# Which engine makes the low halves of the streamed weights: VectorE in place of VectorE and GpSimd in turn

## The chip, the cores and the metric

The kernel runs on one core of a Trainium2 chip. Its time is device microseconds (us) from launch to end. Before the change the median of 3 runs was 2225.28 us (2224.88 to 2227.35). One further execution was profiled and took 2224.93 us. All durations below come from that one.

The engines are named as in the profile: PE is TensorE (PEld its weight loads), DVE is VectorE, ACT is ScalarE, POOL is GpSimd and SP is the engine that issues the loads.

## The reference

Two transformer blocks run on one sequence of 256 tokens with 1024 features, in fp32. The first has two layers: a short-convolution mixer, then windowed attention, each followed by a product-key mixture of experts (PEER). The second block mixes pooling, an mLSTM and a block attention, and ends with a gated feed-forward. The change touches the first convolution mixer and that feed-forward:

```python
def _short_conv_mixer(x, w_in, w_conv, w_out):
    gate_b, gate_c, h = jnp.split(x @ w_in, 3, axis=-1)
    y = conv(gate_c * h, w_conv)          # depthwise, width 3
    return (gate_b * y) @ w_out

# feed-forward of the second block: D_FF = 2816 = 22 * 128
h2 = rmsnorm(x, ln2_g)
u = causal_dwconv(h2 @ w_up, ffn_conv)    # depthwise, width 3
x = x + (silu(u[..., :D_FF]) * u[..., D_FF:]) @ w_down
```

## The kernel before

**Split weights.** Every fp32 weight comes from HBM once, in units of 128 x 1024 (512 KB). Each unit is split into two fp32r tiles: ACT copies `raw` to the high part `wh` (L127), and one of DVE and POOL subtracts, `wl = raw - wh` (L128). The activations are split alike (`xh`, `xl`; `ah`, `al` for the feed-forward's inner values, L186 and L187). A product is then three matmuls into one bank: high by high, high by low, low by high.

**Two shapes of product.** `c_unit` (L153) takes one unit as eight 128 x 128 blocks that stand still while 256 token columns move: 24 matmuls (L159 to L161). `t_mm` (L172) takes a unit as the moving operand, 512 columns at a time, over four banks: 12 matmuls (L177, L178, L181). `t_end` (L204) does the last two units of such a sum in halves (L168 to L170), so that the first half of the tokens ends early.

**Buffers.** `raw` has four, `wh` and `wl` three each. `prepare` (L149) splits up to the third unit behind the one just used, so the split of a unit can start when PE has used up the unit three before it.

**Who makes the low part.** `lo_on["pat"]` is a string, and a counter steps through it: "V" is DVE always, "P" POOL always, "VP" each in turn. Stages set it. Before the change it is "VP" in the convolution mixer (from the end of its first step on) and in the feed-forward. `settle` (one split, L272) and `t_end` override it with "P", and `t_phase` with "V".

**The order.** PE and SP follow the order in which the program is written. The instructions of DVE, ACT and POOL are put in order by the scheduler of the tile layer when the kernel is built. Each engine works through its own list strictly in order.

**The feed-forward.** Step c of 25 makes two `c_unit`s, one for each half of the gate (banks 0 and 1 for even c, 2 and 3 for odd c), and from step 3 on one `t_mm` with the gated result of step c - 3. `up_work` does the work between: for each half a scale by `rbc` that reads the bank (L1136) and three taps (L1139, L1140, L1141), then Silu on ACT (L1143) and the product (L1144). `split_small` splits that product (L186, L187). A full step therefore uses three weight units, and half of their low parts (1.5 on average) are POOL's. Ahead of it, `norm_scales` and `spread` make `rbc`: two DVE scalings of the identity (L328), two matmuls (L329) and a copy (L330).

**The convolution mixer.** Eight steps of three `c_unit`s; `conv_work` (L377 to L384) is its DVE work, seven instructions a step.

Of the kernel before, what the change touches and what calls it, by code (L numbers as in the profile page):

```python
# [40 lines left out]
def kernel(ctx: ExitStack, tc: tile.TileContext, a, out):  # L41
    nc = tc.nc
    V, S, P, T = nc.vector, nc.scalar, nc.gpsimd, nc.tensor
# [48 lines left out]
    lo_on = {"i": 0, "pat": "V"}  # L92
# [60 lines left out]
    def c_unit(out_ps, ahead=True, src=None):  # L153
        h, l = unit()
        ah, al = src or (xh, xl)
        hv = h.rearrange("p (k m) -> p k m", k=8)
        lv = l.rearrange("p (k m) -> p k m", k=8)
        for k in range(8):
            T.matmul(out_ps, hv[:, k], ah[:, k], start=k == 0, stop=False)  # L159
            T.matmul(out_ps, hv[:, k], al[:, k], start=False, stop=False)  # L160
            T.matmul(out_ps, lv[:, k], ah[:, k], start=False, stop=k == 7)  # L161
        if ahead:
            prepare()
# [40 lines left out]
    def t_end(k, n, get, cur, arrive):  # L204

        pat, lo_on["pat"] = lo_on["pat"], "P"
        prepare()
        lo_on["pat"] = pat
        u = [unit()]
        while len(cur) < 2:  # L210
            cur.append(get(k + len(cur)))
        u.append(unit())

        def part(b, nn, q):
            t_half(bank[4 + b * 2 + nn], u[q][0], u[q][1], cur[q][0], cur[q][1], b, nn, k == 0 and q == 0, q == 1)

        for nn in range(2):
            part(0, nn, 0)
            part(0, nn, 1)
        for nn in range(2):  # L220
            arrive(0, nn)
            part(1, nn, 0)
        for nn in range(2):
            part(1, nn, 1)
        for nn in range(2):
            arrive(1, nn)
# [38 lines left out]
    def landing(scale=None, low=False):  # L265
        def arrive(b, n):
            add_x(b, n, scale)
            for c in range(4 * n, 4 * n + 4):
                T.transpose(spot(b, c, low), x[:, b, c * 128:c * 128 + 128], ident)
        return arrive  # L270

    def settle(g, low=False, dst=None):  # L272

        h, l = dst or (xh, xl)
        for b in range(2):
            bs = slice(b * 128, b * 128 + 128)
            for c in range(8):
                i = S.activation(h[:, c, bs], spot(b, c, low), AF.Copy, scale=g[:, c:c + 1])
                V.scalar_tensor_tensor(l[:, c, bs], spot(b, c, low), g[:, c:c + 1], h[:, c, bs],  # L279
                                       op0=ALU.mult, op1=ALU.subtract)  # L280
            if b == 0:
                pat, lo_on["pat"] = lo_on["pat"], "P"
                pump_split(st["use"] + 2)
                lo_on["pat"] = pat
        st["after"] = i
# [79 lines left out]
    def conv_norm():  # L365
        norm_scales()
        spread(bank[7])
        V.tensor_tensor(rb2, rbc, rbc, op=ALU.mult)
# [6 lines left out]
    def conv_work(ct):  # L375
        bs = 4 - 4 * (ct % 2)
        V.tensor_tensor(csb, bank[bs + 1][:, :256], rb2, op=ALU.mult)  # L377
        V.tensor_tensor(u[:, 1:257], bank[bs + 2][:, :256], csb, op=ALU.mult)
        w = [cols[:, C_CONVW + ct * 3 + k:C_CONVW + ct * 3 + k + 1] for k in range(3)]
        V.tensor_scalar(ysb, u[:, 0:256], w[0], None, op0=ALU.mult)  # L380
        V.scalar_tensor_tensor(ysb, u[:, 1:257], w[1], ysb, op0=ALU.mult, op1=ALU.add)
        V.scalar_tensor_tensor(ysb, u[:, 2:258], w[2], ysb, op0=ALU.mult, op1=ALU.add)
        V.tensor_tensor(ysb, ysb, rbc, op=ALU.mult)
        V.tensor_tensor(G[ct], bank[bs][:, :256], ysb, op=ALU.mult)  # L384

    for ct in range(8):
        for g in range(3):
            c_unit(bank[4 - 4 * (ct % 2) + g][:, :256])
            if g == 0 and ct:
                conv_work(ct - 1)  # L390
        if ct == 0:
            lo_on["pat"] = "VP"
            conv_norm()
            T.matmul(bank[3][0:32, :], rb, bk1, start=True, stop=True)
            V.tensor_tensor(mk1, bank[3][0:32, :], mk1, op=ALU.add)
# [399 lines left out]
    def block2():  # L795
# [322 lines left out]
        wo(5)  # L1118
        fetch(7)
        t_end(6, 8, None, cur, landing())  # L1120
        lo_on["pat"] = "VP"
        settle(cols[:, C_LN2:C_LN2 + 8])


# [54 lines left out]
    attention()  # L1179
    peer(1)  # L1180
    block2()


# [120 lines left out]
```

## Time and profile before

| | before |
|---|---|
| median of 3 runs | 2225.28 us |
| profiled execution | 2224.93 us, span 2223.2 us |
| PE busy | 2140.8 us (96%) |
| DVE busy | 1698.7 us (76%) |
| ACT busy | 1144.2 us (51%) |
| POOL busy | 520.7 us (23%) |
| low parts (L128) on DVE | 494, mean 1228 ns |
| low parts (L128) on POOL | 197, mean 2556 ns |
| mean granted TensorE clock | 0.985 |

The span is 1.7 us shorter than the time of the same execution. A share over the whole span mixes stages with different limits: the convolution mixer stands at about 8 to 105 us and the feed-forward at about 2007 to 2219 us, and what matters is read from those two. An engine with a high busy share is not thereby doing useful work all that time: an instruction counts as busy from its start to its end, also while it is held up.

### The profile page before, as it was taken

How to read it: one execution, taken by the hardware profiler on the slowest of the kernel's cores; microseconds unless marked ns; L12 is line 12 of the kernel's file. 1: busy time of each engine (PE TensorE's matmuls, PEld its weight loads, DVE VectorE, ACT ScalarE, POOL GpSimd, SP SyncE). 2: the span in 40 equal slices, each digit the busy share in tenths (PEclk: the TensorE clock that was granted, in tenths of full speed). 3: DMA queues.
4: the chain of work that ended last, by engine and by line, in shares of the span. 5: the costliest groups of instructions: out<-in, count | busy, mean ns of one | idle time of the engine just before them, and what ended most of it. 6: DMA issues, size and time to landing. Idle time of an engine off the chain costs nothing.

```text
span 2223.2 us, 38284 instructions
## 1 busy us (share of the span) xinstructions
PE 2140.8 (96%) x14590; PEld 1945.2 (87%) x14590; DVE 1698.7 (76%) x3048; ACT 1144.2 (51%) x2102; POOL 520.7 (23%) x219
## 2 busy tenths in 40 slices
PE   9999799999999999989998999999999999889998
PEld 9899799999988888877988999998888887768887
DVE  7699968896566666686999788955666666889998
ACT  4455345554555555666544555545555556655333
POOL 3368630000000000144678100000000003533443
PEclk9999899999999999999998999999999999999999
DMA  7686454555667666534454554556676665424553
GB/s 226 181 239 188 133 178 152 155 159 171 205 204 225 209 191 197 173 103 152 144 160 152 166 158 153 156 178 209 196 219 194 193 193 176 124 88 153 168 170 125
DMA packets 109025, 384.45 MB, mean 173 GB/s; under 512 B 11876, under 2 KB 15332, under 8 KB 108584
## 3 DMA queue, kind: packets, MB, share of 16 engines
q1 hardware_dynamic: 108552, 381.81, 55.3%
q8 instruction: 114, 1.87, 0.3%
q14 instruction: 71, 0.58, 0.1%
q10 hardware_dynamic: 288, 0.19, 0.0%
HBM read 374.61 MB, written 7.34 MB: 172 GB/s over the span
## 4 chain that ended last, share of the span: by engine, by line
PE 80%; DVE 12%; issue 4%; POOL 2%; ACT 2%; DMA 0%; SPq 0%; POOLq 0%; ACTq 0%; DVEq 0%
PE bank L159 14%; PE bank L161 13%; PE bank L160 13%; PE bank L177 11%; PE bank L178 11%; PE bank L181 11%; PE bank L533 3%; DVE arena L1141 2%; POOL wl L128 2%; DVE wl L128 2%; DVE arena L1139 1%; ACT wh L127 1%; DVE arena L1140 1%; DVE arena L858 1%; DVE arena L1136 1%
## 5 line engine op out<-in xcount | busy, mean ns | idle before, releaser
L127 ACT ACTIVATE wh<-raw 128x1024 fp32r<-128x1024 f32 x691 | 729.6, 1059 | 370.0 <-PE bank L160 185.5
L159 PE MATMUL bank<-xh,wh 128*128 128x256 f32 x2792 | 808.9, 290 | 18.7 <-ACT arena L554 11.3
L161 PE MATMUL bank<-xh,wl 128*128 128x256 f32 x2792 | 797.3, 286 | 12.4 <-DVE wl L128 10.2
L160 PE MATMUL bank<-xl,wh 128*128 128x256 f32 x2792 | 794.7, 285 | 0.0
L128 DVE TENSOR_TENSOR wl<-raw,wh 128x1024 fp32r<-128x1024 f32 x494 | 606.5, 1228 | 244.5 <-ACT wh L127 244.3
L128 POOL TENSOR_TENSOR wl<-raw,wh 128x1024 fp32r<-128x1024 f32 x197 | 501.7, 2556 | 1051.4 <-ACT wh L127 1000.1
L159 PEld LDWEIGHTS bank<-xh,wh 128*128 128x128 f32 x2792 | 540.1, 193 | 24.6 <-ACT arena L554 12.1
L161 PEld LDWEIGHTS bank<-xh,wl 128*128 128x128 f32 x2792 | 539.6, 193 | 18.7 <-DVE wl L128 13.8
L160 PEld LDWEIGHTS bank<-xl,wh 128*128 128x128 f32 x2792 | 540.5, 194 | 1.5 <-DVE xl L279 0.8
L177 PE MATMUL bank<-wh,ah 128*128 128x512 f32 x1160 | 454.6, 392 | 0.0
L178 PE MATMUL bank<-wl,ah 128*128 128x512 f32 x1160 | 454.1, 391 | 0.2 <-DVE wl L128 0.2
L181 PE MATMUL bank<-wh,al 128*128 128x512 f32 x1160 | 358.2, 390 | 0.0
L186 ACT ACTIVATE ah<-arena 128x256 fp32r<-128x256 f32 x270 | 112.7, 418 | 341.7 <-PE bank L178 279.2
L178 PEld LDWEIGHTS bank<-wl,ah 128*128 128x128 f32 x1160 | 218.8, 189 | 47.6 <-DVE wl L128 2.7
L177 PEld LDWEIGHTS bank<-wh,ah 128*128 128x128 f32 x1160 | 218.8, 189 | 46.6 <-issue 2.1
L181 PEld LDWEIGHTS bank<-wh,al 128*128 128x128 f32 x1160 | 218.5, 188 | 45.8
L187 DVE TENSOR_TENSOR al<-arena,ah 128x256 fp32r<-128x256 f32 x270 | 116.2, 431 | 125.0 <-PE bank L181 110.1
L310 POOL TENSOR_TENSOR top<-x,arena 128x512 f32<-128x512 f32 x4 | 5.1, 1293 | 631.9 <-DVE x L245 631.9
L524 DVE TENSOR_TENSOR x<-iota,ijT 128x1024 f16<-128x1024 f16 x128 | 89.9, 703 | 52.9 <-PE bank L533 52.9
L547 ACT ACTIVATE arena<-bank 128x284 f32<-128x284 f32 (+42 forms) x128 | 38.9, 304 | 130.9 <-DVE arena L545 130.9
L526 DVE TENSOR_TENSOR x<-x,wT 128x1024 f16<-128x1024 f16 x128 | 96.6, 756 | 0.0
L533 PE MATMUL bank<-x 128*128 128x128 f16 x1024 | 81.2, 220 | 0.0
(296 smaller groups left out, 2056.8 us busy)
## 6 DMA issues: line engine op xcount, KB each, us to landing
raw<-in_u_dram SPq DMA_DIRECT2D x256, 512.0 KB, 3.5
raw<-in_v_dram SPq DMA_DIRECT2D x256, 512.0 KB, 3.5
raw<-in_ff_dram SPq DMA_DIRECT2D x66, 512.0 KB, 3.5
raw<-in_wq_dram SPq DMA_DIRECT2D x32, 512.0 KB, 4.0
raw<-in_conv_in_dram SPq DMA_DIRECT2D x23, 512.0 KB, 4.1
raw<-in_conv_out_dram SPq DMA_DIRECT2D x8, 512.0 KB, 3.6
f_d<-arena SPq DMA_DIRECT2D x8, 512.0 KB, 7.2
raw<-in_aq_dram SPq DMA_DIRECT2D x8, 512.0 KB, 3.5
```

The lines of the kernel that those rows point to most:

```text
L127: S.activation(h, r, AF.Copy)
L128: (P if pat[lo_on["i"] % len(pat)] == "P" else V).tensor_sub(l, r, h)
L159: T.matmul(out_ps, hv[:, k], ah[:, k], start=k == 0, stop=False)
L160: T.matmul(out_ps, hv[:, k], al[:, k], start=False, stop=False)
L161: T.matmul(out_ps, lv[:, k], ah[:, k], start=False, stop=k == 7)
L177: T.matmul(bank[4 + b * 2 + n], sh[:, bs], h[:, ns], start=first, stop=False)
L178: T.matmul(bank[4 + b * 2 + n], sh[:, bs], l[:, ns], start=False, stop=False)
L181: T.matmul(bank[4 + b * 2 + n], sl[:, bs], h[:, ns], start=False, stop=last)
L186: S.activation(h, src, AF.Copy)
L187: V.tensor_sub(l, src, h)
L526: V.tensor_tensor(W, E[:, 1:2].to_broadcast(shape), wT[:, c, :, :, None, :].to_broadcast(shape), op=ALU.mult)
L533: T.matmul(bk[:, t * 128:t * 128 + 128], E[:, 0, t // 2, :, t % 2], W[:, q, t // 2, :, t % 2], start=q == 0, stop=q == 1)
```

## The change

Two settings of the pattern change. The one of the convolution mixer is taken out, so that the pattern keeps its first value "V"; the one ahead of the feed-forward becomes "V".

```diff
         if ct == 0:
-            lo_on["pat"] = "VP"
             conv_norm()
...
         t_end(6, 8, None, cur, landing())
-        lo_on["pat"] = "VP"
+        lo_on["pat"] = "V"
         settle(cols[:, C_LN2:C_LN2 + 8])
```

Since a line falls away, the lines after L391 have a number lower by one in the new kernel: its L1138 is the L1139 of before.

In the DVE's list the last full step of the feed-forward (`up_work(21)`, banks 2 and 3) stood like this; `wl` is a low part of a weight unit, `al` that of the activations, `arena` the working memory:

```order
2404 L1136 TENSOR_TENSOR arena<-bank_94,rbc 128x256
2405 L1139 TENSOR_SCALAR arena<-arena,cols 128x256
2406 L1140 SCALAR_TENSOR_TENSOR arena<-arena,cols 128x256
2407 L1141 SCALAR_TENSOR_TENSOR arena<-arena,cols 128x256
2408 L1136 TENSOR_TENSOR arena<-bank_95,rbc 128x256
2409 L1139 TENSOR_SCALAR arena<-arena,cols 128x256
2410 L1140 SCALAR_TENSOR_TENSOR arena<-arena,cols 128x256
2411 L128 TENSOR_TENSOR wl<-raw,wh 128x1024
2412 L1141 SCALAR_TENSOR_TENSOR arena<-arena,cols 128x256
2413 L1144 TENSOR_TENSOR arena<-arena 128x256
2414 L187 TENSOR_TENSOR al<-arena,ah 128x256
```

In the new list the same step, from its second instruction on, is:

```order
2448 L1138 TENSOR_SCALAR arena<-arena,cols 128x256
2449 L1139 SCALAR_TENSOR_TENSOR arena<-arena,cols 128x256
2450 L128 TENSOR_TENSOR wl<-raw,wh 128x1024
2451 L1140 SCALAR_TENSOR_TENSOR arena<-arena,cols 128x256
2452 L1135 TENSOR_TENSOR arena<-bank_95,rbc 128x256
2453 L1138 TENSOR_SCALAR arena<-arena,cols 128x256
2454 L128 TENSOR_TENSOR wl<-raw,wh 128x1024
2455 L1139 SCALAR_TENSOR_TENSOR arena<-arena,cols 128x256
2456 L1140 SCALAR_TENSOR_TENSOR arena<-arena,cols 128x256
2457 L1143 TENSOR_TENSOR arena<-arena 128x256
2458 L128 TENSOR_TENSOR wl<-raw,wh 128x1024
2459 L187 TENSOR_TENSOR al<-arena,ah 128x256
```

Every step now has three low parts in the DVE's list: one between the taps of the first half, one between those of the second, and one between the product and `al`. Before, steps had two and one in turn.

On POOL, the end of the list was as follows (L1015 to L1018 are the pooling mixer):

```order
19 L1015 TENSOR_TENSOR top<-top 64x256
20 L1016 COPY top<-top 64x256
21 L1017 TENSOR_TENSOR top<-top,arena 128x2x256
22 L1018 TENSOR_TENSOR top<-top,arena 128x2x256
23 L128 TENSOR_TENSOR wl<-raw,wh 128x1024 x33
```

and is now:

```order
19 L1014 TENSOR_TENSOR top<-top 64x256
20 L1015 COPY top<-top 64x256
21 L1016 TENSOR_TENSOR top<-top,arena 128x2x256
22 L1017 TENSOR_TENSOR top<-top,arena 128x2x256
23 L128 TENSOR_TENSOR wl<-raw,wh 128x1024
```

32 of the 33 low parts have left POOL; the one that stays is `settle`'s. Near the start of the same list a run of 143 becomes one of 132: 11 low parts of the convolution mixer have left as well. In that mixer, two steps of the DVE's list were:

```order
34 L384 TENSOR_TENSOR arena<-bank_96,arena 128x256
35 L187 TENSOR_TENSOR al<-arena,ah 128x256
36 L377 TENSOR_TENSOR arena<-bank_93,arena 128x256
37 L128 TENSOR_TENSOR wl<-raw,wh 128x1024
38 L378 TENSOR_TENSOR arena<-bank_94,arena 128x256
39 L380 TENSOR_SCALAR arena<-arena,cols 128x256
40 L381 SCALAR_TENSOR_TENSOR arena<-arena,cols 128x256
41 L382 SCALAR_TENSOR_TENSOR arena<-arena,cols 128x256
42 L383 TENSOR_TENSOR arena<-arena,rbc 128x256
43 L384 TENSOR_TENSOR arena<-bank_92,arena 128x256
44 L128 TENSOR_TENSOR wl<-raw,wh 128x1024
45 L187 TENSOR_TENSOR al<-arena,ah 128x256
```

and are now:

```order
34 L128 TENSOR_TENSOR wl<-raw,wh 128x1024
35 L384 TENSOR_TENSOR arena<-bank_96,arena 128x256
36 L377 TENSOR_TENSOR arena<-bank_93,arena 128x256
37 L128 TENSOR_TENSOR wl<-raw,wh 128x1024
38 L187 TENSOR_TENSOR al<-arena,ah 128x256
39 L378 TENSOR_TENSOR arena<-bank_94,arena 128x256
40 L380 TENSOR_SCALAR arena<-arena,cols 128x256
41 L381 SCALAR_TENSOR_TENSOR arena<-arena,cols 128x256
42 L128 TENSOR_TENSOR wl<-raw,wh 128x1024
43 L382 SCALAR_TENSOR_TENSOR arena<-arena,cols 128x256
44 L383 TENSOR_TENSOR arena<-arena,rbc 128x256
45 L384 TENSOR_TENSOR arena<-bank_92,arena 128x256
```

A low part has moved in ahead of the last product (L384), and one between the taps. The lists of PE and SP are the same as before; ACT's holds the same instructions, some of the feed-forward's in another order.

## Rows read from the trace of the kernel before

**Rows 1.** Stretches: length, busy us and count of each engine, granted clock, DMA.

```profile
core 0: us, PE busy (x) PEld busy (x) DVE busy (x) ACT busy (x) POOL busy (x), PEclk, DMA share, GB/s
20.00:82.00 62.00, 62.00 (x510) 60.99 (x509) 47.03 (x69) 23.52 (x25) 24.41 (x10) 1.00 0.62 185
...
2018.00:2031.90 13.90, 13.90 (x118) 13.90 (x117) 13.87 (x27) 6.82 (x10) 5.12 (x2) 1.00 0.46 152
2034.70:2195.80 161.10, 150.96 (x1021) 136.93 (x1020) 151.26 (x202) 63.02 (x86) 66.40 (x27) 1.00 0.54 167
2195.80:2208.00 12.20, 11.78 (x74) 10.10 (x73) 11.62 (x17) 4.17 (x7) 5.47 (x2) 1.00 0.29 88
2208.00:2219.20 11.20, 7.78 (x25) 5.40 (x24) 6.44 (x7) 1.29 (x2) 2.44 (x1) 0.85 0.12 47
2212.60:2217.50 4.90, 4.86 (x14) 3.80 (x15) 1.81 (x3) 0.00 (x0) 0.00 (x0) 0.65 0.15 56
```

**Rows 2.** Waits from 2034.7 us on: waiter, whom for, us, times, longest.

```profile
PEld bank L161 <- DVE wl L128: 13.8, 18, 0.9
...
PEld bank L168 <- ACT ah L186: 3.1, 1, 3.1
```

**Rows 3.** Groups by line, 2034.7 to 2195.8 us: busy us, mean ns.

```profile
L128 POOL TENSOR_TENSOR wl<-raw,wh 128x1024 fp32r<-128x1024 f32 x27 | 71.9, 2663 | 99.4 <-ACT wh L127 58.1 <-DVE al L187 32.7 <-DVE arena L1139 4.8
...
L1141 DVE SCALAR_TENSOR_TENSOR arena<-arena,cols 128x256 f32<-128x256 f32 x35 | 49.0, 1399 | 0.6
L128 DVE TENSOR_TENSOR wl<-raw,wh 128x1024 fp32r<-128x1024 f32 x26 | 31.7, 1221 | 1.8 <-ACT wh L127 1.8
...
L1139 DVE TENSOR_SCALAR arena<-arena,cols 128x256 f32<-128x256 f32 x35 | 27.0, 772 | 1.1
...
L1140 DVE SCALAR_TENSOR_TENSOR arena<-arena,cols 128x256 f32<-128x256 f32 x36 | 23.5, 653 | 1.1
...
L1136 DVE TENSOR_TENSOR arena<-bank,rbc 128x256 f32<-128x256 f32 x34 | 14.2, 417 | 0.0
...
L1144 DVE TENSOR_TENSOR arena<-arena 128x256 f32<-128x256 f32 x18 | 7.6, 424 | 1.2
L187 DVE TENSOR_TENSOR al<-arena,ah 128x256 fp32r<-128x256 f32 x18 | 7.6, 422 | 4.0 <-ACT ah L186 3.9
```

**Rows 4.** Single lines, 2034.7 to 2195.8 us: shortest, median and longest ns.

```profile
L1141 DVE SCALAR_TENSOR_TENSOR arena<-arena,cols x35: 470/485/2626, 2035.7 to 2190.3; 128x256 f32<-128x256 f32 x35
...
L1139 DVE TENSOR_SCALAR arena<-arena,cols x35: 342/354/2196, 2035.4 to 2194.6; 128x256 f32<-128x256 f32 x35
...
L1140 DVE SCALAR_TENSOR_TENSOR arena<-arena,cols x36: 473/485/2616, 2033.2 to 2195.0; 128x256 f32<-128x256 f32 x36
```

**Rows 5.** Timelines of POOL and DVE near the end: start us, duration us.

```profile
2195.77 3.11 POOL L128 TENSOR_TENSOR wl<-raw,wh 128x1024 fp32r<-128x1024 f32 x1 [3.17 <-ACT wh L127]
...
2196.55 2.62 DVE L1141 SCALAR_TENSOR_TENSOR arena<-arena,cols 128x256 f32<-128x256 f32 x1
...
2202.94 2.40 POOL L128 TENSOR_TENSOR wl<-raw,wh 128x1024 fp32r<-128x1024 f32 x1 [4.06 <-DVE al L187]
...
2203.30 2.18 DVE L1139 TENSOR_SCALAR arena<-arena,cols 128x256 f32<-128x256 f32 x1
```

**Rows 6.** PE's timeline over the last units.

```profile
2205.28 0.39 PE L177 MATMUL bank<-wh,ah 128*128 128x512 f32 x1
...
2208.01 0.47 PE L168 MATMUL bank<-wh,ah 128*128 128x512 f32 x1
...
2212.64 0.51 PE L168 MATMUL bank<-wh,ah 128*128 128x512 f32 x1 [2.66 <-ACT ah L186]
...
2218.94 0.40 PE L170 MATMUL bank<-wh,al 128*128 128x512 f32 x1
```

**Rows 7.** Timelines of DVE and PE where `rbc` is made.

```profile
2016.61 0.28 DVE L328 TENSOR_SCALAR gt<-ident,sm 128x128 f32<-128x128 f32 x1
...
2017.12 0.61 PE L329 MATMUL bank<-gt,ones 128*128 128x128 f32 x4
```

**Rows 8.** One tap of the convolution mixer: shortest, median, longest ns.

```profile
L382 DVE SCALAR_TENSOR_TENSOR arena<-arena,cols x8: 481/1494/2587, 25.8 to 83.7; 128x256 f32<-128x256 f32 x8
```

## The prediction

> **What bounds the kernel now.** First the stretches [rows 1], since the two stages that change have different limits. In the convolution mixer (20 to 82 us) PE is busy for all 62.0 us and DVE for 47.0: PE is the limit, and it waits for no one. In the feed-forward (2034.7 to 2195.8 us, 17 steps, 1020 matmuls) PE is busy 151.0 of 161.1 us and DVE 151.3: here DVE is as full as PE, and PE has gaps. Next, who causes them: PE's weight loads of L161 wait 13.8 us in 18 waits for a low part that DVE makes, and behind the last step one wait of 3.1 us is for ACT's `ah` [rows 2]. So the feed-forward is bound by DVE. POOL's own low parts are hardly ever waited for.
>
> Then, what fills DVE [rows 3, 4]. The tap L1141 takes 485 ns in the median and 2626 ns at most; L1139 354 and 2196; L1140 485 and 2616. The same instruction on the same shape is either short or some 2 us longer. The timelines say when [rows 5]: POOL's low part runs from 2195.77 to 2198.88, and L1141 from 2196.55 to 2199.17, done 0.29 us after POOL. POOL's next runs from 2202.94 to 2205.34, and L1139 from 2203.30 to 2205.48, done 0.14 us after it. A tap that begins while POOL subtracts ends when POOL ends. L1136, which reads a bank, has a mean of 417 ns and is never long [rows 3].
>
> The sum of the stretching: L1141 49.0 - 35 x 0.485 = 32.0 us, L1139 27.0 - 35 x 0.354 = 14.6, L1140 23.5 - 36 x 0.485 = 6.0, together 52.6 us of DVE time. POOL's group holds 27 instructions, one cut off by the edge of the stretch, so 26 to 27 share it: 2.0 us each. A low part that DVE makes itself costs it 1.221 us [rows 3]. Taken from DVE to POOL to spare DVE 1.2 us, a low part costs DVE 2.0.
>
> The Trainium skill has a rule for this, in "SBUF — State Buffer", section "Who interferes with whom": a DVE instruction with two inputs in SBUF, or in a two-port mode, and a GpSimd instruction that reads SBUF exclude each other, and the one that comes second is blocked until the first is done. By that rule L1136, with one input in PSUM, should escape and the taps should not, and the trace agrees (417 ns mean against 2626 at most). Another of its rules speaks against the change: "Perfetto Trace Analysis", section "Optimizing Scalar/DVE Operations", says that where DVE is saturated, handing work to ScalarE or even GpSimd may make sense. By that rule alone, taking work back to a DVE that is busy 151 of 161 us makes the kernel slower; that is the last rival below. The same section adds that between these two engines it might not help.
>
> **The change, part by part.** *DVE in the feed-forward.* A full step now holds three low parts. From the short durations [rows 3, 4]: two halves at 0.417 + 0.354 + 0.485 + 0.485 = 1.741 us make 3.48; the product 0.424 and `al` 0.422 make 0.85; three low parts at 1.221 make 3.66. That is 7.99 us. What PE needs for a step: in 2018.0 to 2031.9 us, where it runs without a gap, 118 matmuls (two of them cut by the edges, so 116) take 13.9 us, 0.120 each [rows 1]; the 12 matmuls of a `t_mm` take from 2205.28 to 2208.01, 0.2275 each [rows 6]. 48 x 0.120 + 12 x 0.2275 = 5.76 + 2.73 = 8.49 us. The step of before took 161.1 / 17 = 9.48. DVE at 7.99 falls below PE at 8.49, so PE becomes the limit, with 0.5 us of a step to spare on DVE.
>
> *Steady steps:* 17 x (9.48 - 8.49) = 16.8 us go. *The last step and the product behind it* (2195.80 to 2208.00): 48 x 0.120 + 24 x 0.2275 = 11.22 us against 12.20, so 1.0 us.
>
> *The tail.* From 2208.01 to the last matmul at 2218.94 there are 23 intervals [rows 6]; at 0.2275 they would take 5.23 us, and took 10.93. The 5.7 us are the wait for the low part of unit 64, the 2.66 us for `ah` of the last product, and the clock behind that wait: granted 0.65 on average from 2212.6 to 2217.5 us [rows 1], so between its two levels of 1.2 and 2.4 GHz, after PE had stood still. These waits exist because DVE is behind. When it is not, the last chain starts with the last `c_unit`: L1136 0.42, L1139 0.35, low part 1.22, L1140 and L1141 0.97, product 0.42, then `ah` on ACT. That is 3.4 us plus what ACT has ahead of it in its list, the high part of the last unit, which cannot start before PE has left the unit three earlier, 2.73 us behind the `c_unit`; so `ah` comes at about 4.3 us. PE wants it after two `t_mm`s and three matmuls, 27 x 0.2275 = 6.1 us. It is 1.8 us early, so the whole tail goes: 5.7 us. The clock has then no standstill to fall for.
>
> *What is added.* Ahead of `rbc` one more low part (unit 3's) stands in DVE's list. The second L328 ended at 2016.89 and PE came to L329 at 2017.12 [rows 7]: cover of 0.23 us. PE then waits between 0 (where the low part falls into time in which DVE waited anyway) and 1.22 - 0.23 = 1.0 us; I take the middle, 0.5. After that DVE starts some steps late, as it does now, and with 0.5 us a step to spare it catches up only over many; a few waits for a low part will remain in the first steps. Their bounds are 0 and, at the 0.77 us of a wait now (13.8 / 18), one per step for five steps, 3.9 us. I take 1.4, a little nearer to the lower end, since the low parts are made two units ahead of their use (about 5.7 us) and a delay under 3 us costs nothing.
>
> What is queued behind a low part that waits for ACT's `wh`: the next tap, Silu and the product, and for these PE waits only three steps later. DVE waited 1.8 us in all for `wh` in the whole stretch [rows 3]. The loads of `raw` are set free by the subtraction, which on DVE ends sooner than on POOL; three units of 0.524 MB in 8.49 us are 185 GB/s, and the mixer already draws 185 [rows 1]. I cost it at nothing.
>
> *Convolution mixer.* DVE gets 11 low parts, 13.4 us, and loses the stretching (L382 alone has a median of 1494 ns against a shortest of 481, [rows 8]), about 2.0 us for each. It stays near 47 of 62 us and PE near 62 of 62: 0, bounds 0 (PE has no wait to win) and 2 us (two low parts late by one subtraction each).
>
> **The sum:** 16.8 + 1.0 + 5.7 = 23.5 us less; 0.5 + 1.4 = 1.9 us more; net 21.6. From the profiled 2224.93 us this gives 2203.3. The median is 0.35 us above the profiled time, so 2203.7; I say 2204. A measurement tells 0.2%, 4.5 us, from no change.
>
> **The rivals.**
> *The tail stays.* ACT's list puts high parts ahead of Silu and `ah` at the end; if the last chain is late by more than its 1.8 us, PE waits again and the clock falls again. For it: the margin is that of one low part and a half. Against it: each piece is priced from rows. It gives 2203.7 + 5.7 = 2209.4. Chance 0.15.
> *Half the gain.* DVE's 0.5 us a step is eaten by waits for `wh`, by its order: a mean of 0.33 us for each of three low parts takes DVE to 8.98 us, half of the way back to 9.48, and the tail stays too. 2203.7 + 8.4 + 5.7 - 1.4 = 2216. For it: three waits a step where there were 1.5. Against it: 1.8 us of such waits over 26 now, 0.07 each. Chance 0.08.
> *No change.* The gaps come back as waits for ACT or a load: 2225. Against it: ACT is busy 63.0 of 161.1 us and DMA 0.54 [rows 1]. Chance 0.03. That the change does nothing is excluded by POOL's list, which is 43 low parts shorter.
> *Slower.* The long taps are DVE's own, because each follows a low part, and do not go with POOL's work. Then DVE adds 26 x 1.221 = 31.7 us to 151.3 and needs 183 us where 161.1 were: 22 us more, and about 2 for the steps around, 2249. This decides from the point where a subtraction taken off POOL gives DVE back less than the 1.22 us it costs there; rows say 2.0. For it: L1141 does stand behind a low part in [rows 5]. Against it: L1139 in the same rows does not, and both end with POOL's instruction. Chance 0.05.
>
> **How the numbers follow.** The forecast, 0.69, has a range of its own from 2202 (nothing left over: 2225.28 - 23.5) to 2207 (both added terms at their upper bounds). To hold 8 in 10 the range must take in the first rival and its remainders: 2202 to 2211. Faster by over 0.2%: forecast 0.69, tail 0.15, half 0.08, less a little for what lies near the bound, 0.91. Same 0.04, slower 0.05.
>
> **What would show it.** Right: no tap of 2 us in the feed-forward; DVE busy about 130 us (151.3 - 52.6 + 31.7) over 17 steps of about 8.5 us; PE's waits for a low part of DVE nearly gone; no wait of PE for `ah` at the end, and a granted clock of 1.0 through the tail; the mixer's stretch unchanged with PE at 62 of 62. Wrong: taps that stay long with POOL idle, a row of waits of DVE for `wh`, or low parts on DVE that take over 1.4 us.

## The result: 1.1% faster, as forecast

| | before | changed |
|---|---|---|
| median | 2226.20 us (5 runs) | 2203.01 us (5 runs) |
| range | 2224.88 to 2227.35 | 2201.73 to 2204.09 |
| profiled span | 2223.2 us | 2200.0 us |
| PE busy | 96% | 97% |
| DVE busy | 1698.7 us | 1675.0 us |
| POOL busy | 520.7 us | 409.1 us |

The ratio is 0.9892, with a 95% interval of 0.9880 to 0.9903: 23.2 us less, where 21.6 was worked out and 2204 forecast. DVE has 43 instructions more and is busy for 24 us less.

The stretches of the changed kernel that answer to [rows 1] (columns as there: length, then PE, PEld, DVE, ACT and POOL busy with counts, granted clock, DMA). The feed-forward's stretches end earlier and hold the same matmuls:

```profile
20.00:82.00 62.00, 62.00 (x511) 61.04 (x511) 49.46 (x79) 23.80 (x25) 0.00 (x0) 1.00 0.60 190
...
2034.70:2179.20 144.50, 144.50 (x1022) 136.16 (x1021) 130.99 (x230) 65.51 (x88) 0.00 (x0) 1.00 0.60 187
2179.20:2190.50 11.30, 11.30 (x74) 10.34 (x73) 10.14 (x18) 5.16 (x7) 0.00 (x0) 1.00 0.18 53
2190.50:2196.20 5.70, 5.63 (x25) 4.32 (x23) 2.31 (x5) 0.00 (x0) 0.00 (x0) 1.00 0.24 92
```

Read against [rows 1] one stretch at a time. The mixer (20 to 82 us): PE 62.0 of 62.0 in both, nothing won, nothing lost. The 17 steps: 161.1 us before, 144.5 now, 8.50 a step, with PE busy throughout. The last step: 12.2 and 11.3. The tail: 11.2 and 5.7, at a clock of 1.00 where 0.85 was granted. Together 16.6 + 0.9 + 5.5 = 23.0 us of the span's 23.2.

The lines of the taps, shortest, median and longest ns (numbers lower by one than in [rows 4]):

```profile
L1138 DVE TENSOR_SCALAR arena<-arena,cols x35: 345/353/356, 2035.8 to 2177.2; 128x256 f32<-128x256 f32 x35
...
L1139 DVE SCALAR_TENSOR_TENSOR arena<-arena,cols x36: 473/480/488, 2035.4 to 2178.9; 128x256 f32<-128x256 f32 x36
...
L1140 DVE SCALAR_TENSOR_TENSOR arena<-arena,cols x37: 474/480/486, 2035.0 to 2176.3; 128x256 f32<-128x256 f32 x37
```

The medians are within 5 ns of those of [rows 4]; the long ones are gone. The instructions have the same shapes and operands; what changed is POOL's work beside them and their place among the low parts. The waits from 2034.7 us on (waiter, whom for, total us, times, longest; "issue" where the profile shows no one that was waited for) are no longer PE's on DVE, as in [rows 2]:

```profile
ACT wh L127 <- issue: 55.3, 38, 1.5
ACT wh L127 <- PE bank L160: 26.3, 15, 1.8
DVE wl L128 <- ACT wh L127: 7.8, 33, 0.6
...
DVE arena L1135 <- PE bank L161: 2.9, 15, 0.5
...
ACT ah L186 <- DVE arena L1143: 0.3, 1, 0.3
```

Where the profile names someone, ACT waits for PE to give back a weight buffer, and DVE waits for ACT's high part and for PE's banks; PE itself is busy for all 144.5 us. That is what a PE-bound stage looks like: the others are ahead and held back by PE.

### The profile page after: what moved, and what is told of

The parts are those of the page before. It is cut to its first block, busy times and chain, and to the rows that moved or that the text cites. A ratio compares the mean times of both kernels' runs of the same rounds, so it can differ in the third digit from the quotient of the medians.

```text
span 2200.0 us, 38262 instructions
## 1 busy us (share of the span) xinstructions
PE 2131.1 (97%) x14590; PEld 1943.2 (88%) x14590; DVE 1675.0 (76%) x3091; ACT 1145.7 (52%) x2102; POOL 409.1 (19%) x176
## 4 chain that ended last, share of the span: by engine, by line
PE 88%; DVE 5%; issue 3%; POOL 2%; ACT 1%; DMA 1%; POOLq 0%; SPq 0%; ACTq 0%
PE bank L159 15%; PE bank L161 15%; PE bank L160 15%; PE bank L177 12%; PE bank L178 12%; PE bank L181 12%; PE bank L532 3%; POOL wl L128 2%; DVE arena L857 1%; ACT wh L127 1%; PE bank L429 0%; DMA x_d<-x 0%; PE bank L735 0%; DVE x L243 0%; DVE wl L128 0%
## 5 line engine op out<-in xcount | busy, mean ns | idle before, releaser
L128 DVE TENSOR_TENSOR wl<-raw,wh 128x1024 fp32r<-128x1024 f32 x537 | 659.1, 1227 | 256.0 <-ACT wh L127 255.3
L159 PE MATMUL bank<-xh,wh 128*128 128x256 f32 x2792 | 808.9, 290 | 19.0 <-ACT arena L553 11.3
L128 POOL TENSOR_TENSOR wl<-raw,wh 128x1024 fp32r<-128x1024 f32 x154 | 390.4, 2547 | 959.7 <-ACT wh L127 957.7
L546 ACT ACTIVATE arena<-bank 128x284 f32<-128x284 f32 (+42 forms) x128 | 38.8, 303 | 131.0 <-DVE arena L544 131.0
```

The lines of the kernel that those rows point to most:

```text
L128: (P if pat[lo_on["i"] % len(pat)] == "P" else V).tensor_sub(l, r, h)
```

## The experiments

The theory: a subtraction on POOL holds up a DVE instruction that reads two inputs from SBUF, or a TENSOR_SCALAR from SBUF to SBUF such as L1139 of before (one input, 2196 ns at most), for some 2.0 us, which costs time where DVE limits. The expectations call the second case the two-port mode; the runs show that it is held, not in which mode it ran. The rivals: the gain is a matter of DVE's new order; POOL's low parts were late as such; DVE's long taps were its own.

### Which of the two places: the mixer or the feed-forward

```diff
 # e1_mixer_only, against the changed kernel: the feed-forward's setting
-        lo_on["pat"] = "V"
+        lo_on["pat"] = "VP"
...
 # e2_ffn_only, against the changed kernel: the mixer's setting
         if ct == 0:
+            lo_on["pat"] = "VP"
```

> Only the convolution mixer's low parts go to DVE; the feed-forward keeps VP. Theory (a low part on POOL costs DVE 2 us of blocking, which matters only where DVE limits): PE is busy without a gap in the mixer before and after, so the time is that of before, 2226 within 2 us. Rival (the new order of DVE's list and the earlier start help everywhere, or low parts pay per piece): 11 of the 43 moved pieces are the mixer's, so 11/43 of the 23 us, 6 us less, 2220.

> Only the feed-forward's low parts go to DVE; the mixer keeps VP. Theory: the whole gain, 2203 within 2 us. Rival (per piece): 32/43 of the gain, 2209.

Measured: 2226.3 us for the mixer alone, ratio 1.000 (0.9991 to 1.001), and 2202.9 us for the feed-forward alone, 0.9891 (0.9875 to 0.9908). The 11 pieces of the mixer are worth nothing that these runs can tell (the interval is 2 us to either side) and the 32 of the feed-forward are worth everything, so the gain does not go by the piece. In the mixer the holds were there as well [rows 8], and in e1 they are gone (the same tap, a line number lower; shortest, median, longest):

```profile
L381 DVE SCALAR_TENSOR_TENSOR arena<-arena,cols x7: 483/485/485, 25.4 to 74.7; 128x256 f32<-128x256 f32 x7
```

The time did not follow, because DVE had 15 us of 62 to spare there.

### POOL at work, with DVE's list untouched

```diff
 # e3_pool_reads
                 cur.append(split_small(gg[(c - 2) % 4]))
+                P.tensor_tensor(ar(100, 4).rearrange("p (k t) -> p k t", k=4), xh[:, 0:4].bitcast(F32),
+                                cur[-1][0].bitcast(F32)[:, None, :].to_broadcast([128, 4, 256]), op=ALU.subtract)
 # e4_pool_writes
                 cur.append(split_small(gg[(c - 2) % 4]))
+                S.activation(ar(100, 4)[:, 0:1], cur[-1][0].bitcast(F32)[:, 0:1], AF.Copy)
+                P.memset(ar(100, 8), 0.0)
```

> The changed kernel, and in each of 21 steps of the feed-forward GpSimd subtracts 128x1024 elements that it reads from SBUF (xh and ah) into a part of the working memory that nothing uses; no one waits for it, and DVE's and ACT's lists are word for word those of the changed kernel. Theory (a DVE instruction that needs two inputs or the two-port mode waits until POOL is done): one stretch of some 2 us a step takes DVE from 7.99 to about 10.0 us a step, above PE's 8.49, so about 1.5 us in each of 18 steps, 27 us, plus the tail's 5.7: 2230 to 2236. Rival (the gain came from the new order of DVE's list, or from POOL's late low parts, not from POOL's running beside DVE): 2203, and no DVE instruction longer than before.

> As the kernel with reads beside it, but GpSimd only writes: it sets 128x2048 elements of unused memory to zero in each of 21 steps (ACT writes one column of it first, to set the pace). Theory (it is the shared way for reads that the taps and POOL contend for): instructions with two SBUF inputs (L1139, L1140, low parts) keep their short durations; at most L1138, which has one input, may be held up; 2203 to 2208. Rival (any work on POOL slows DVE, by its writes or otherwise): stretched taps of two inputs as with reads, and a time between 2215 and 2236.

With the reads: 2233.1 us (2229.5 to 2236.5, 8 runs), ratio 1.0029 (1.0019 to 1.004). A subtraction that nobody waits for takes back the whole gain and more. POOL's and DVE's timelines (start, duration, line):

```profile
2108.80 2.75 POOL L1174 TENSOR_TENSOR arena<-xh,ah 128x1024 f32<-128x1024 f32 x1 [7.02 <-ACT ah L186]
```

```profile
2108.06 1.22 DVE L128 TENSOR_TENSOR wl<-raw,wh 128x1024 fp32r<-128x1024 f32 x1
2109.20 2.63 DVE L187 TENSOR_TENSOR al<-arena,ah 128x256 fp32r<-128x256 f32 x1
2111.76 0.41 DVE L1135 TENSOR_TENSOR arena<-bank,rbc 128x256 f32<-128x256 f32 x1
```

Here it is `al` that is held, the next instruction with two SBUF inputs after POOL starts; before it was a tap. It ends at 2111.83, 0.28 us after POOL at 2111.55. In some of the earlier steps POOL's subtraction meets a tap, and then L1139 (2626 ns at most) or L1140 (2622) is the long one; L1135, which reads a bank, is never above 422 ns. For `al` over the stretch from 2034.7 to 2180 us (shortest, median, longest):

```profile
L187 DVE TENSOR_TENSOR al<-arena,ah x17: 409/2630/2639, 2035.0 to 2177.6; 128x256 fp32r<-128x256 f32 x17
```

From 2093.26 to 2200.77 us the first matmuls of 12 successive steps lie 9.77 us apart, where the theory said about 10.0 and the changed kernel has 8.50. The lists of DVE and ACT are the changed kernel's to the word, so the new order cannot be the cause of the gain, and the long instructions are not DVE's own. The rivals that it is order, and that the long taps are DVE's own, fall here.

With the writes: 2202.5 us (two runs), ratio 0.9889 (0.9869 to 0.9909), and the taps with two inputs are as short as in the changed kernel (shortest, median, longest; then the group of the memsets: busy, mean):

```profile
L1138 DVE TENSOR_SCALAR arena<-arena,cols x35: 336/354/1108, 2036.3 to 2177.7; 128x256 f32<-128x256 f32 x35
```

```profile
L1139 DVE SCALAR_TENSOR_TENSOR arena<-arena,cols x36: 464/478/487, 2035.9 to 2179.4; 128x256 f32<-128x256 f32 x36
```

```profile
L1175 POOL MEMSET arena<- 128x2048 f32 x18 | 32.6, 1808 | 109.1 <-ACT arena L1174 109.1
```

```profile
2105.25 1.81 POOL L1175 MEMSET arena<- 128x2048 f32 x1 [6.69 <-ACT arena L1174]
```

```profile
2105.77 0.42 DVE L187 TENSOR_TENSOR al<-arena,ah 128x256 fp32r<-128x256 f32 x1
```

`al`, held for 2.2 us by a subtraction, passes in 0.42 us beside a memset that runs from 2105.25 to 2107.06. So POOL's being busy is not what holds a two-input instruction. That it is the reading is the nearest reading of the contrast; no run has POOL read without also computing. The Trainium skill ("SBUF — State Buffer", "Who interferes with whom") states that a DVE instruction with two SBUF inputs contends with a GpSimd instruction that reads SBUF, and not with one that only writes it. The runs agree: 2.63 us beside the subtraction, 0.42 beside the memset.

L1138, which has one input, is another matter. It was long twice, 1.11 us and, at 2081.37, 0.71; both times it began while a memset ran and ended 0.15 us after it. The first:

```profile
2042.94 1.81 POOL L1175 MEMSET arena<- 128x2048 f32 x1 [9.57 <-ACT arena L1174]
```

```profile
2043.79 1.11 DVE L1138 TENSOR_SCALAR arena<-arena,cols 128x256 f32<-128x256 f32 x1
```

So work on POOL that only writes can hold a TENSOR_SCALAR, as the expectation allowed; here it was rare, since L1138 seldom came while much of a memset was left.

### One low part in three

```diff
-        lo_on["pat"] = "V"
+        lo_on["pat"] = "VVP"
         settle(cols[:, C_LN2:C_LN2 + 8])
```

> The changed kernel, but in the feed-forward GpSimd makes every third low part (pattern VVP; before it was every second). Theory (each costs DVE 2.0 us of blocking where its own would cost 1.22): DVE's step is 3.48 + 0.85 + 2 x 1.22 + 2.0 = 8.8 us against PE's 8.49, so 0.3 us in each of 18 steps and a tail that is again a little late: 2207 to 2214, well below half-way back. Rival (a low part on POOL is simply late for PE, each by as much): 22 of 33 pieces, two thirds of the way back, 2218.

Measured: 2207.3 us, 0.9910 (0.9894 to 0.9927). In the stretch from 2034.7 to 2180 us nearly all of the holding falls on one line, L1138, whose instruction has a single input (busy us, mean ns):

```profile
L1138 DVE TENSOR_SCALAR arena<-arena,cols 128x256 f32<-128x256 f32 x35 | 42.0, 1201 | 1.1
L128 DVE TENSOR_TENSOR wl<-raw,wh 128x1024 fp32r<-128x1024 f32 x34 | 41.5, 1222 | 2.8 <-ACT wh L127 2.8
L128 POOL TENSOR_TENSOR wl<-raw,wh 128x1024 fp32r<-128x1024 f32 x16 | 38.7, 2417 | 100.8 <-ACT wh L127 100.8
...
L1140 DVE SCALAR_TENSOR_TENSOR arena<-arena,cols 128x256 f32<-128x256 f32 x36 | 19.5, 541 | 0.6
```

L1138 was held for 42.0 - 35 x 0.353 = 29.6 us and one L1140 for 19.5 - 36 x 0.48 = 2.2, together 31.8 us over 16 subtractions, 2.0 each. 21 of the 32 pieces that the change moved are back on POOL here (POOL has 175 low parts, the changed kernel 154). They cost 4.3 us, and the other 11 cost 19. Lateness by the piece would have cost two thirds of 23, so that rival falls too.

The time lies at the lower end of the expectation. The steady steps are 8.59 us apart (by their first matmuls), where 8.8 was worked out: DVE's own step of 7.99 us was too large. The changed kernel shows 131.0 / 17 = 7.71, and from there 7.71 - 1.22 + 2.0 = 8.49 is an estimate of DVE's step here, just PE's. So the steep part of the loss begins about where DVE's step passes PE's.

### The tail by itself

```diff
-        lo_on["pat"] = "V"
+        lo_on["pat"] = "VP"
         settle(cols[:, C_LN2:C_LN2 + 8])
...
         for c in range(25):
+            if c == 19:
+                lo_on["pat"] = "V"
```

> The feed-forward with VP as before up to step 18, and DVE alone from step 19 on: the steady loss without the tail's. Theory: most of the steady steps' 16.8 us comes back (15 of 17 steps, 14.8 us), while DVE, freed for the last steps, is hardly late for the last chain, so of the tail's 5.7 us little or nothing returns: 2217 to 2220. Rival (the tail has its own cause, the order of ACT's list at the end): tail stall of 3 us with the low clock, 2223 or more.

Measured: 2218.3 us, 0.9961 (0.9945 to 0.9977). The stretches (as in [rows 1]): the steps with POOL, the last two and what follows, the tail:

```profile
2034.70:2187.00 152.30, 142.98 (x965) 129.50 (x964) 143.35 (x192) 59.31 (x81) 62.09 (x24) 1.00 0.54 168
2187.00:2206.70 19.70, 19.70 (x133) 18.27 (x132) 19.04 (x35) 9.62 (x13) 0.00 (x0) 1.00 0.43 140
2206.70:2212.40 5.70, 5.61 (x25) 4.32 (x23) 2.71 (x6) 0.00 (x0) 0.00 (x0) 1.00 0.24 92
```

The steps are lost as before, and the tail takes 5.7 us at a granted clock of 1.00 all the same. POOL's last low part ended at 2180.59, so about three steps without POOL are enough to work the lateness off.

This run alone does not acquit the order of the lists, since with the new pattern at the end the last instructions of ACT's and DVE's lists stand in the order of the changed kernel and not in that of before. The run with the reads tells more, since its DVE and ACT lists are the changed kernel's throughout. There the starts of the last 24 matmuls span 8.9 us, where the changed kernel and this run have 5.2 and the kernel before 10.9; PE waits 0.70 us for `ah` and 1.99 for the last `al`, which POOL holds for 2.57. So the new order does not by itself free the tail; a late DVE delays it in that order too. How much of the 10.9 of before was due to the old order is not separated.

### Where else POOL makes low parts

```diff
 # e7_peer_V: both expert stages
-        lo_on["pat"] = "P"
+        lo_on["pat"] = "V"
         st["ready"] = 0
...
 # e8_block2_V: the second block's mLSTM and attention
-        lo_on["pat"] = "P"
+        lo_on["pat"] = "V"
         c_unit(bank[2][:, :256])
...
 # e9_attention_V: the windowed attention; e10_attention_block2_V has this edit and that of e8
         settle(cols[:, C_ATTNG:C_ATTNG + 8])
-        lo_on["pat"] = "P"
+        lo_on["pat"] = "V"
```

> The changed kernel, and DVE also makes the 112 low parts that GpSimd has in the two expert stages while DVE selects the top 16. DVE is busy there 99 of 100 us; its work is mostly MAX8, FIND_INDEX8 and the like, which read one input, so the stretching by POOL is about 0.7 us a low part (40.9 us for 43 from 107 to 260 us, a quarter of it no stretching). Theory (moving pays where the stretch exceeds 1.22 us): about 0.5 us lost for each of some 70 that fall where DVE limits, 20 to 50 us slower, 2223 to 2253. Rival (POOL's low parts always cost more than DVE's own): faster than 2203.

> The changed kernel, and DVE also makes 15 low parts of the second block's mLSTM and attention stage (1890 to 1990 us), where the stretching comes to 26.4 us for 21, about 1.25 each, much like the 1.22 a low part costs DVE. Theory: break-even, 2203 within 4 us. Rival (always a gain): 2185 to 2198.

> The changed kernel, and DVE also makes 17 low parts of the windowed attention (930 to 1040 us), where the stretching comes to 15.8 us for 13, about 1.2 each. Theory (moving pays only where the stretch is above 1.22 us and DVE limits): within 3 us of the changed kernel, 2200 to 2206. Rival (always a gain): 2190 to 2198.

> The changed kernel with both the attention's and the second block's remaining low parts on DVE. Theory: near break-even again, 2198 to 2206; if both stages have a small gain it is the fastest version, 1 to 4 us below the changed kernel beside it. Rival (always a gain): below 2195.

> The changed kernel itself, on the same chip as the two beside it: 2203 within 2 us by every theory; it is what those two are compared with.

| kernel | median | ratio to before (95%) |
|---|---|---|
| e7, expert stages | 2213.9 us | 0.9943 (0.9927 to 0.9960) |
| e8, second block | 2201.1 us | 0.9879 (0.9861 to 0.9898) |
| e9, attention | 2197.5 us | 0.9868 (0.9851 to 0.9884) |
| e10, both | 2193.0 us | 0.9854 (0.9835 to 0.9874) |
| e11, the changed kernel | 2202.7 us | 0.9896 (0.9880 to 0.9913) |

In the expert stages the same exchange loses: 11 us slower than the changed kernel. That DVE's own low parts are always the better choice is excluded. The expected 20 to 50 us were too much: I took the holding at 0.7 us a piece and 70 pieces where DVE limits; which of the two was wrong, these runs don't tell apart. DVE is full there, but about half of its time goes to MAX8, FIND_INDEX8 and their kin (49 us of the 100 from 1100 to 1200), and those are not held (one MAX8 line of the changed kernel; shortest, median, longest):

```profile
L442 DVE MAX8 arena<-top x32: 396/406/428, 169.1 to 1134.9; 128x8 f32<-128x256 f32 x32
```

The second block alone (e8) came within the expected 4 us of 2203, and its interval overlaps that of the changed kernel.

The expectation for e9 (2200 to 2206) and e10 (2198 to 2206) was wrong on the other side. e10 is faster by 9.7 us than the changed kernel on the same chip (e11), and the two intervals do not meet; e9 is 5.3 us faster, with intervals that just overlap. Break-even in DVE's busy time was the wrong measure there, since in attention DVE is not full: 72.0 of 95 us from 945 to 1040 in e11. The changed kernel (e11's trace) at 1000 us, on POOL, DVE, PE's waits from 990 to 1016, and the stretch with its granted clock:

```profile
1000.50 2.35 POOL L128 TENSOR_TENSOR wl<-raw,wh 128x1024 fp32r<-128x1024 f32 x1 [5.32 <-ACT wh L127]
```

```profile
1000.55 2.32 DVE L723 TENSOR_TENSOR arena<-arena 128x4 f32<-128x4 f32 x1 [0.30 <-ACT arena L719]
1002.79 1.21 DVE L712 TENSOR_REDUCE arena<-arena 128x4 f32<-128x1024 f32 x1
1003.92 0.41 DVE L755 TENSOR_TENSOR top<-arena,top 128x256 fp32r<-128x256 f32 x1
```

```profile
PE bank L701 <- DVE top L755: 3.9, 2, 3.0
```

```profile
1000.00:1012.00 12.00, 8.12 (x34) 6.42 (x34) 9.02 (x23) 5.14 (x16) 2.35 (x1) 0.72 0.14 44
```

L723 adds four numbers a partition and takes 0.14 us seven microseconds later; here it is held for 2.32. Two places behind it in DVE's list is L755, for which PE stands still for 3.0 us; then the clock falls, to 0.72 on average over these 12 us, which lies between its two levels of 1.2 and 2.4 GHz. In e10 the same place, where PE's waits for L755 come to 0.4 us:

```profile
1000.26 0.15 DVE L723 TENSOR_TENSOR arena<-arena 128x4 f32<-128x4 f32 x1
```

```profile
996.00:1006.00 10.00, 9.18 (x66) 6.48 (x64) 9.95 (x32) 6.83 (x23) 0.00 (x0) 1.00 0.17 52
```

Counted by the start of the same matmul in both traces, e10 goes from 0.2 us behind at 989 us to 7.1 us ahead at 1017 (the 6675th and the 6825th matmul), nearly all of it at this one place. e9 gains the same 7.3 us between these two matmuls, and e8, which leaves the attention alone, gains nothing there; e8 and e10 gain another 2.9 in the second block. So these 7.3 us go with the attention's low parts. That the hold of L723 is the whole of it is read from this trace; no run took that one hold away alone.

## Why the prediction was right

**The limit.** The feed-forward was bound by DVE, and DVE by POOL's reads: e3 puts the reads back and the time with them, e4 shows that a POOL that only writes costs nothing here, and the taps fell to their short durations.

**The steps.** 16.8 us were worked out from 9.48 against 8.49 a step; 16.6 came (8.50 a step). The last step: 1.0 and 0.9. DVE's busy time over the 17 steps: about 130 forecast, 131.0 measured. The other figure for DVE, 7.99 us a step, would make 135.8 over 17 steps and was too large: it adds whole durations, while successive DVE instructions overlap at their ends (in e3's rows the low part of 2108.06 ends at 2109.28, and `al` begins at 2109.20). DVE had 0.8 us of a step to spare and not 0.5.

**The tail.** 5.7 worked out, 5.5 came, clock 1.00. The last `ah` was expected 4.3 us behind the last `c_unit`; DVE's and ACT's rows give the chain, with PE's last `c_unit` ending as its next matmul starts at 2185.07:

```profile
2185.20 1.06 ACT L127 ACTIVATE wh<-raw 128x1024 fp32r<-128x1024 f32 x1 [1.82 <-PE bank L160]
2186.16 0.40 ACT L1142 ACTIVATE arena<-arena 128x256 f32<-128x256 f32 x1
2188.06 1.06 ACT L127 ACTIVATE wh<-raw 128x1024 fp32r<-128x1024 f32 x1 [1.50 <-issue]
2189.03 0.40 ACT L186 ACTIVATE ah<-arena 128x256 fp32r<-128x256 f32 x1
```

`ah` is done at 2189.43, 4.36 us behind; PE took it up at 2191.21. The rival in which the tail stays is out: with DVE on time the last `ah` was 1.8 us early, as worked out.

**The mixer.** 0 forecast; e1 measures a ratio of 1.000, within 2 us.

**The two terms that were too large.** For the start I added 0.5 us and for late low parts of the first steps 1.4. Neither came: from 2005 us on no wait of PE for a low part of DVE is left. The added low part ahead of `rbc` ran from 2012.64 to 2013.87, and before, DVE had waited 1.36 us for ACT at that place; the second L328 ended at 2016.99 and PE came at 2017.23. The wait in the kernel before, then the new rows:

```profile
2013.14 0.15 DVE L297 TENSOR_SCALAR sm<-sm 128x1 f32<-128x1 f32 x1 [1.36 <-ACT junk L237]
```

```profile
2012.64 1.23 DVE L128 TENSOR_TENSOR wl<-raw,wh 128x1024 fp32r<-128x1024 f32 x1 [0.76 <-ACT wh L127]
```

```profile
2016.71 0.28 DVE L328 TENSOR_SCALAR gt<-ident,sm 128x128 f32<-128x128 f32 x1
```

```profile
2017.23 0.61 PE L329 MATMUL bank<-gt,ones 128*128 128x128 f32 x4
```

The lower bounds, 0, would have given 2201.8 (2225.28 - 23.5), and against the median of before over five runs, 2226.2, 2202.7; 2203.0 was measured. The three terms of the gain were right, 23.5 us for 23.2; the 1.9 us that were added for safety were not needed, and the larger spare time of DVE's step says why late low parts did not show.

**The rival of half the gain.** It named waits of DVE for `wh` of 0.33 us on each low part. There were 33 of them from 2034.7 us on, 0.24 us each, and PE had no gap beside them: DVE has these waits because it is ahead, so they fill the spare time of its step and take nothing from PE. The prediction had named a row of such waits as a sign of being wrong. The row came with the forecast time, so that sign did not separate the cases.

## What to carry to other kernels

A high busy share says that instructions were in flight, not that the engine worked: compare the median of a line with its longest before calling an engine full, and look on the other engine for what ends when the long ones end. Work handed from VectorE to GpSimd that reads SBUF is paid for by whatever instruction VectorE comes to next that can be held: in these traces one with two SBUF inputs, or a TENSOR_SCALAR on SBUF. It paid where VectorE was full and much of its work could not be held (MAX8 and its kin in the expert stages), and it cost where VectorE was the limit and each step held such instructions (the feed-forward), or where, as the trace suggests, a tiny instruction on the way to TensorE was the one that was caught (the attention). A moved unit of work is worth nothing where the engine that it frees was not the limit (the mixer), so find the stage first and change only that.

## What the runs showed of the hardware that was not expected

The hold does not scale with the instruction held: one that takes 0.14 us was held for 2.32 us by a subtraction of 2.35 us. A memset of 128 x 2048 on GpSimd (1.81 us) left VectorE's two-input instructions at their short times (L1139 at most 487 ns), but it held the one-input L1138 twice, to 1.11 and 0.71 us against a median of 0.35.
